# The last pair's pooled mixture loaded in parts, one of them straight from SBUF, with the value steps queued behind the first output products

## The chip, the cores and the metric

One NeuronCore of a Trainium2 chip runs the whole layer. The metric is device microseconds of one execution. The engines keep their own names here: PE (TensorE matmul) with its weight loads (PEld), DVE (VectorE), ACT (ScalarE), POOL (GpSimd) and SP (SyncE, which here only issues DMAs). Each engine has one placed order of instructions; that order is what the change moves.

## The reference, cut to what matters

One decoder layer over 1024 tokens of width 1024, all in float32:

```python
h = x @ w_in                           # columns: pool | q | k | v | forget gate
pool_out = pool_mixer(u, pool_w, pool_scale)      # 4 channel groups, trailing means over 2, 4, 8, 16 tokens
attn_out = forgetting_attention(q, k, v, f_logit) # 8 heads of 64, causal, decay bias
x = layer_norm(alpha * x + concat(pool_out, attn_out) @ w_out)
x = layer_norm(alpha * x + square(relu(x @ w_mlp1)) @ w_mlp2)
```

`concat(pool_out, attn_out)` is called the mixture here. It has 8 channel groups of 128: groups 0 to 3 are the pooled ones, groups 4 to 7 are the four pairs of heads.

## The kernel before, in words

A float32 product is made of three fast ones: every operand is split into a high part (an ACT copy that rounds) and a low part (a DVE subtraction), and `three` issues high x high, high x low, low x high (lines 83 to 85). Products of 512 columns into one PSUM bank are the unit of PE's work.

The mixture goes through a DRAM tensor, `mix_dram`, laid out as four blocks of 256 tokens; each block holds for 128 partitions 8 groups x 256 tokens. Pooled groups 1 to 3 ("early") are written there long before the last pair of heads. Pooled group 0 ("late", window 2) is computed in two halves of 512 tokens (`late_group`), each followed by its small linear map (`late_linear`, line 466: three products, an ACT scaling into the tile `mx`, a store to `mix_dram` at line 471).

Attention runs over pairs of heads, in blocks of 256 queries. A unit of it has two parts: `att_probs` (scores on PE at lines 369, 370 and 372, a running minimum on DVE at line 375, the exponent on ACT at line 377) and `att_values` (transposes at line 397, a high copy on ACT at 398, a low subtraction on DVE at 399, value products at 416, then a store of the result at 423). The units are pipelined by one: values of one unit stand between the probabilities of the next.

Between these steps `fillstep` draws other PE work from a generator, at a rate that spreads the pieces over the last eight units. For the last pair (units with p = 3) the generator is `last_fill` (line 475): the late pooled group in two halves, the loads of the output weights `w_out` (lines 512 and 516), then `mixture(0, 0)` and `mixture(0, 1)` (line 521: a load of four groups of one block, for half 1 also two loads of the softmax row scales from `rin_dram` at line 529 and a DVE multiplication at line 530, then a split), then the output products of the first two token tiles (`out_proj`, line 535): for each tile eight `three`s that need half 0 of the mixture (k = 0 to 3, for both halves of the columns) and eight that need half 1 (k = 4 to 7). `normed` (line 552) adds the residual and normalises; its square root needs another ACT table than the exponent.

A scheduler places all instructions, engine by engine, from its own idea of their durations, so the order on an engine isn't that of the source text. SBUF slots come from small rings by tag (S 3, U 2, B 14, Q 10, A 9): a tile that reuses a slot waits for the last reader of the tile before.

Of the kernel before, what the change touches and what calls it, by code (L numbers as in the profile page):

```python
# [1 line left out]

# [34 lines left out]
def trunk(ctx, tc, xT, xn, wuqk, wvf, bf, poolw, pscale, wout, g1, b1, w1, w2, g2, b2, out):  # L37
# [43 lines left out]
    def three(dst, a, b, first, last):  # L81

        nc.tensor.matmul(dst, a[0], b[0], start=first, stop=False)
        nc.tensor.matmul(dst, a[0], b[1], start=False, stop=False)
        nc.tensor.matmul(dst, a[1], b[0], start=False, stop=last)


    ident = small([P, P], "ident")
# [291 lines left out]
    def att_values(p, e, m, prob, ahead):  # L380
        h = 2 * p + e
        rows = slice(e * HD, (e + 1) * HD)
        orow = slice((1 - e) * HD, (2 - e) * HD)
        ov = bank("pv")[:, 0:256]

        def turned(jp):
            tp = bank("pt")
            tt = slot("A", [2, CH])
            if jp < m:
                blocks = [(jj * 256 + ii * P, 2 * jp + jj, ii) for jj in range(2) for ii in range(2)]  # L390
                ev = slice(0, CH)
            else:
                blocks = [(P, 2 * jp + 1, 1), (2 * P, 2 * jp, 0), (3 * P, 2 * jp, 1)]
                ev = slice(P, CH)
                nc.gpsimd.memset(tt[:, :, 0:P].bitcast(F32), 0.0)
            for col, j, ii in blocks:
                nc.tensor.transpose(tp[:, col : col + P], prob[ii][:, j * P : (j + 1) * P], ident)  # L397
            nc.scalar.copy(tt[:, 0, ev], tp[:, ev])  # L398
            nc.vector.tensor_tensor(tt[:, 1, ev], tp[:, ev], tt[:, 0, ev].bitcast(F32), ALU.subtract)  # L399
            return tt  # L400

        nxt = turned(0)
        next(ahead, None)
        for jp in range(m + 1):
            tt = nxt
            if jp < m:
                nxt = turned(jp + 1)
            if jp == (m + 1) // 2:
                run(ahead)
            fillstep()  # L410
            mov = ((0, 256), (256, CH)) if jp < m else ((256, CH), (0, 256))
            for s in range(2):
                for jj in range(2):
                    j = 2 * jp + jj
                    a, b = mov[jj]
                    nc.tensor.matmul(  # L416
                        ov, V[j][:, h].rearrange("p s d -> p (s d)"), tt[:, s, a:b],
                        start=(j == 0 and s == 0), stop=(j == 2 * m + 1 and s == 1),
                    )
        mx = slot("U", [256], F32)  # L420
        nc.scalar.copy(mx[rows], ov[orow])
        nc.vector.tensor_tensor(mx[rows], ov[rows], mx[rows], ALU.add)
        nc.sync.dma_start(mix_dram[m, rows, NG + p, :], mx[rows])
        if p == NPAIR - 1:
            row_scales(h, 2 * m, 2)
        elif m == 0:
            row_scales(h, 0, NT)
# [37 lines left out]

    def late_linear(c, pw):
        y, mx = pooled.pop(c)
        dst = bank("mm")
        three(dst, (pw[:, 0], pw[:, 1]), (y[:, 0], y[:, 1]), True, True)
        nc.scalar.activation(mx, dst, AF.Copy, scale=half_scale)  # L470
        nc.sync.dma_start(
            mix_dram[2 * c : 2 * c + 2, :, LATE, :].rearrange("m p t -> p m t"), mx.rearrange("p (m t) -> p m t", m=2)
        )

    def last_fill():
        w = load_w(wuqk[LATE])
        st = slot("S", [P], F32)
        nc.sync.dma_start(st, poolw[:, LATE])
        pw = slot("U", [2, P])
        split(pw[:, 0], pw[:, 1], st)  # L480
        nc.vector.tensor_scalar(half_scale, ps_sb[:, LATE : LATE + 1], 0.5, None, ALU.mult)
        yield from late_group(0, w)
        load_output_weights(0, 4)
        yield from late_group(1, w)
        late_linear(0, pw)
        yield
        load_output_weights(4, KT)
        load_rows()
        mixture(0, 0)
        mixture(0, 1)  # L490
        pair = slot("B", [2, D], F32)
        for t in range(2):
            xt = pair[:, t]
            nc.sync.dma_start(xt, xn[t])
            yp = [bank("mm") for n in range(2)]
            for half in range(2):
                yield from out_proj(t, yp, range(4 * half, 4 * half + 4))
                if t == half == 0:
                    late_linear(1, pw)
                    yield  # L500
            normed(t, xt, yp)

    wo = {}
# [13 lines left out]
                wo[block] = (hi[:, k], lo[:, k])  # L517

    mixes, done = {}, []

    def mixture(m, half):

# [12 lines left out]
    def out_proj(t, yp, ks):  # L535
        ts_ = slice((t % 2) * P, (t % 2 + 1) * P)
        for n, part in enumerate(yp):
            ns = slice(n * CH, (n + 1) * CH)
            for k in ks:
                a, w = mixes[t // 2, k // 4], wo[k]  # L540
                three(part, (a[0][:, k % 4, ts_], a[1][:, k % 4, ts_]), (w[0][:, ns], w[1][:, ns]), k == 0, k == KT - 1)
                yield

    gb = []

# [16 lines left out]
    class Norm:  # L562
# [53 lines left out]
        def by_three(self):  # L616
# [4 lines left out]
            for c, x in zip(self.cols, self.x):  # L621
# [2 lines left out]
                nc.gpsimd.tensor_tensor(y, y, self.gam[:, c], ALU.mult)  # L624
                nc.gpsimd.tensor_tensor(y, y, self.bet[:, c], ALU.add)
                nc.sync.dma_start(self.store[:, c], y)
    fill = {"gen": iter(()), "credit": 0.0, "rate": 0.0}

    def fillstep():
        fill["credit"] += fill["rate"]  # L630
        while fill["credit"] >= 1.0:
            fill["credit"] -= 1.0
            next(fill["gen"], None)

    order = [(p, e, m) for p in range(NPAIR - 1) for e in range(2) for m in (3, 2, 1, 0)]
    order += [(NPAIR - 1, e, m) for m in range(4) for e in range(2)]
# [622 lines left out]
```

## Time and profile before

| what | us |
|---|---|
| median of 3 runs | 1039.18 (1038.84 to 1039.32) |
| the profiled execution, its own time | 1040.64 |
| its span from the first to the last instruction | 1038.9 |
| PE busy | 1018.5 (98%) |
| DVE busy | 756.6 (73%) |
| ACT busy | 513.6 (49%) |
| POOL busy | 155.0 (15%) |

The profiled execution is 1.46 us slower than the median of the runs; its span leaves 1.74 us outside. Times inside the trace count from the span's start. In the rows of a timeline stand: start, duration, engine, line, operation, output and inputs with the buffer numbers left out, the count of merged instructions, and in brackets how long the engine was idle before and what ended that. The rows of a view by stages hold, for each engine, busy time and count of instructions.

### The profile page before, as it was taken

How to read it: one execution, taken by the hardware profiler on the slowest of the kernel's cores; microseconds unless marked ns; L12 is line 12 of the kernel's file. 1: busy time of each engine (PE TensorE's matmuls, PEld its weight loads, DVE VectorE, ACT ScalarE, POOL GpSimd, SP SyncE). 2: the span in 40 equal slices, each digit the busy share in tenths (PEclk: the TensorE clock that was granted, in tenths of full speed). 3: DMA queues.
4: the chain of work that ended last, by engine and by line, in shares of the span. 5: the costliest groups of instructions: out<-in, count | busy, mean ns of one | idle time of the engine just before them, and what ended most of it. 6: DMA issues, size and time to landing. Idle time of an engine off the chain costs nothing.

```text
span 1038.9 us, 14121 instructions
## 1 busy us (share of the span) xinstructions
PE 1018.5 (98%) x4976; PEld 846.5 (81%) x4976; DVE 756.6 (73%) x1300; ACT 513.6 (49%) x823; POOL 155.0 (15%) x267
## 2 busy tenths in 40 slices
PE   9999999999989999999999999999999999999996
PEld 9988887888767888787888888888878888888884
DVE  4777678677767887989888778788885666565547
ACT  4523566666665332676666766768621211122152
POOL 0200112112100031112122122120100000000047
PEclk9999999999999999999999999999999999999998
DMA  9702311111584532139767567565999888878753
GB/s 359 273 28 82 111 65 32 36 47 54 173 281 140 185 122 99 61 125 353 275 229 276 224 253 273 217 265 184 346 316 321 283 258 283 275 222 269 242 186 121
DMA packets 113671, 206.30 MB, mean 199 GB/s; under 512 B 9592, under 2 KB 78008, under 8 KB 113600
## 3 DMA queue, kind: packets, MB, share of 16 engines
q1 hardware_dynamic: 94608, 137.63, 40.5%
q0 software_dynamic: 18560, 67.12, 16.7%
q8 instruction: 39, 0.64, 0.2%
q10 hardware_dynamic: 432, 0.66, 0.2%
q14 instruction: 32, 0.26, 0.1%
HBM read 132.42 MB, written 72.94 MB: 198 GB/s over the span
## 4 chain that ended last, share of the span: by engine, by line
PE 49%; issue 4%; DVE 3%; DMA 2%; POOL 1%; ACT 0%; DVEq 0%; POOLq 0%; SPq 0%
PE s L1060 15%; PE pv L1060 8%; PE s L727 8%; PE mm L727 6%; PE pt L727 6%; PE pv L727 4%; PE pt L1060 2%; PE mm L1060 2%; DMA S<-in_w_dram 2%; DVE B L72 1%; DMA hid_dram<-A 1%; POOL hid_dram L852 0%; POOL A L720 0%; DVE A L850 0%; DVE bns L573 0%
## 5 line engine op out<-in xcount | busy, mean ns | idle before, releaser
L71 ACT CAST B<-S 128x1024 fp32r<-128x1024 f32 (+1 forms) x78 | 67.7, 881 | 169.4 <-DMA S<-in_w_dram 67.5
L727 PE MATMUL s<-B,Q 128*128 128x512 f32 x492 | 116.4, 389 | 0.2 <-ACT B L71 0.2
L727 PEld LDWEIGHTS s<-B,Q 128*128 128x128 f32 x492 | 92.3, 188 | 19.8 <-ACT B L71 0.6
L72 DVE TENSOR_TENSOR B<-S,B 128x1024 fp32r<-128x1024 f32 (+1 forms) x78 | 78.0, 1008 | 34.0 <-ACT B L71 33.9
L1060 PE MATMUL s<-B,Q 128*128 128x512 f32 x402 | 98.2, 390 | 0.0
L1060 PEld LDWEIGHTS s<-B,Q 128*128 128x128 f32 x402 | 75.5, 188 | 16.2
L71 ACT CAST Q<-S 128x1024 fp32r<-128x1024 f32 x53 | 55.7, 1051 | 58.0 <-PE s L727 17.0
L852 POOL DMA_DIRECT2D hid_dram<-A x90 | 48.1, 537 | 221.5 <-ACT A L849 164.6
L1060 PE MATMUL s<-B,A 128*128 128x512 f32 x321 | 79.7, 393 | 0.0
L72 DVE TENSOR_TENSOR Q<-S,Q 128x1024 fp32r<-128x1024 f32 x53 | 65.6, 1238 | 15.3 <-ACT Q L71 14.8
L727 PE MATMUL pt<-B,Q 128*128 128x512 f32 x312 | 74.6, 389 | 0.0
L727 PE MATMUL mm<-B,Q 128*128 128x512 f32 x300 | 71.6, 389 | 0.0
L1060 PEld LDWEIGHTS s<-B,A 128*128 128x128 f32 x321 | 60.3, 188 | 13.5
L727 PEld LDWEIGHTS pt<-B,Q 128*128 128x128 f32 x312 | 58.5, 188 | 12.1
L727 PEld LDWEIGHTS mm<-B,Q 128*128 128x128 f32 x300 | 56.3, 188 | 11.7
L377 ACT ACTIVATE A<-A,nm 128x1024 f32<-128x1024 f32 (+7 forms) x64 | 49.7, 778 | 32.3 <-DVE nm L375 31.1
L416 PE MATMUL pv<-A,B 128*128 128x256 f32 x320 | 62.2, 295 | 2.7 <-DVE A L399 1.3
L416 PEld LDWEIGHTS pv<-A,B 128*128 128x128 f32 x320 | 51.0, 188 | 17.1 <-ACT A L398 6.9
L399 DVE TENSOR_TENSOR A<-pt,A 128x512 fp32r<-128x512 f32 (+1 forms) x80 | 49.6, 634 | 15.2 <-ACT A L398 14.4
L850 DVE TENSOR_TENSOR A<-A,A 128x1024 f32<-128x1024 f32 x45 | 53.6, 1219 | 0.0
L362 POOL TENSOR_TENSOR A<-A,maskb 128x128 f32<-128x128 f32 x48 | 23.5, 492 | 190.8 <-DVE nm L375 131.8
L398 ACT CAST A<-pt 128x512 fp32r<-128x512 f32 (+1 forms) x80 | 41.4, 542 | 19.3 <-PE pt L397 18.4
(427 smaller groups left out, 2341.7 us busy)
## 6 DMA issues: line engine op xcount, KB each, us to landing
hid_dram<-A POOLq DMA_DIRECT2D x105, 512.0 KB, 4.0
S<-in_w_dram SPq DMA_DIRECT2D x62, 512.0 KB
Q<-hid_dram SPq DMA_DIRECT2D x98, 256.0 KB
A<-hid_dram SPq DMA_DIRECT2D x82, 256.0 KB
S<-in_wuqk_dram SPq DMA_DIRECT2D x12, 512.0 KB
wo_dram<-Q POOLq DMA_DIRECT2D x10, 512.0 KB, 3.8
B<-wo_dram SPq DMA_DIRECT2D x10, 512.0 KB
Q<-hid_dram SPq DMA_DIRECT2D x39, 128.0 KB
```

The source lines that it names most:

```text
L71: nc.scalar.copy(hi, src)
L72: nc.vector.tensor_tensor(lo, src, hi.bitcast(F32), ALU.subtract)
L362: nc.gpsimd.tensor_tensor(nb[:, qs], nb[:, qs], maskb, ALU.add)
L377: nc.scalar.activation(pt[:, :nk], pt[:, :nk], AF.Exp, bias=nm, scale=-1.0, accum_out=rsum[h][:, i : i + 1])
L398: nc.scalar.copy(tt[:, 0, ev], tp[:, ev])
L399: nc.vector.tensor_tensor(tt[:, 1, ev], tp[:, ev], tt[:, 0, ev].bitcast(F32), ALU.subtract)
L416: nc.tensor.matmul(ov, V[j][:, h].rearrange("p s d -> p (s d)"), tt[:, s, a:b], start=(j == 0 and s == 0), stop=(j == 2 * m + 1 and s == 1),)
L727: nc.tensor.matmul(dst, b[x][:, k], A[a][y][:, k], start=first and k == 0 and i == 0, stop=k == H - 1 and i == 2, skip_group_check=not first,)
L850: nc.vector.tensor_tensor(x, x, hi.bitcast(F32), ALU.subtract)
L852: nc.gpsimd.dma_start(hid_dram[self.u, :, i, AT[name] : AT[name] + 2 * CH], part.rearrange("p q n t -> p (q n t)"))
L1060: nc.tensor.matmul(dst, h[:, p_], w[q_], start=first and u == self.us[0] and j == 0, stop=u == self.us[-1] and j == 2, skip_group_check=no ...
```

## The change

- `last_fill` now calls `early_mixture` at its start: groups 1 to 3 of half 0 of the first token block are loaded and split at once (768 columns), into tiles made for all four groups.
- `late_linear(0)` is called inside the second half of the late group, after five of its eight pieces, and no longer behind it. It splits the first 256 columns of its result from `mx`, in SBUF, into group 0 of those tiles; the store to `mix_dram` stays, since the second token block still reads it. So `mixture(0, 0)` is gone as a load.
- `late_linear(1)` takes a PSUM bank of the scores (`s`, 3 banks) in place of one of `mm` (2 banks).
- `mixture(0, 1)` is called behind `late_linear(1)`, after the first eight output pieces.
- `three` returns its last instruction, `out_proj` yields it, and `fillstep` keeps the latest of the first eight that it sees. The value products of an attention step are then placed behind that instruction on PE: an order on the same engine, no semaphore.

```diff
@@ three
-        nc.tensor.matmul(dst, a[1], b[0], start=False, stop=last)
+        return nc.tensor.matmul(dst, a[1], b[0], start=False, stop=last).ins
@@ att_values
-            for s in range(2):
-                ...
+            with tc.issue_after(fill["piece"]) if fill["piece"] else nullcontext():
+                for s in range(2):
+                    ...
@@ late_linear
-        dst = bank("mm")
+        dst = bank("s" if c else "mm")
...
+        if c == 0:
+            hi, lo = mixes[0, 0]
+            split(hi[:, LATE], lo[:, LATE], mx[:, 0:256])
@@ last_fill
+        early_mixture()
         yield from late_group(0, w)
         load_output_weights(0, 4)
-        yield from late_group(1, w)
-        late_linear(0, pw)
-        yield
+        for n, _ in enumerate(late_group(1, w)):
+            yield
+            if n == 4:
+                late_linear(0, pw)
+                yield
         load_output_weights(4, KT)
         load_rows()
-        mixture(0, 0)
-        mixture(0, 1)
...
                 if t == half == 0:
                     late_linear(1, pw)
                     yield
+                    mixture(0, 1)
@@ new
+    def early_mixture():
+        mf = slot("S", [4, 256], F32)
+        nc.sync.dma_start(mf[:, 1:4], mix_dram[0, :, 1:4, :])
+        hi, lo = slot("Q", [4, 256]), slot("Q", [4, 256])
+        split(hi[:, 1:4], lo[:, 1:4], mf[:, 1:4])
+        mixes[0, 0] = (hi, lo)
@@ out_proj
-                three(part, ...)
-                yield
+                yield three(part, ...)
@@ fillstep
-            next(fill["gen"], None)
+            piece = next(fill["gen"], None)
+            if piece and fill["pieces"] < 8:
+                fill["piece"], fill["pieces"] = piece, fill["pieces"] + 1
```

Where the placed order differs, place one: PE in the first units of the last pair, a few rows behind the small linear map of the first late half. In a row stand the line, the operation, the output tile, its inputs and the size; `s` are scores, `pt` transposes, `pv` values, `mm` with B and Q inputs are output products (B a weight, Q the mixture). Before:

```order
L397 MATMUL pt_3307<-ident_63,A_3206 128x128
L397 MATMUL pt_3307<-ident_63,A_3180 128x128
L397 MATMUL pt_3307<-ident_63,A_3206 128x128
L369 MATMUL s_3326<-Q_2364,Q_2365 128x512
L416 MATMUL pv_3285<-A_3287,B_389 128x256 x2
L370 MATMUL s_3326<-Q_2364,Q_2366 128x512
L369 MATMUL s_3331<-Q_2364,Q_2365 128x256
L370 MATMUL s_3331<-Q_2364,Q_2366 128x256
L372 LDWEIGHTS identb_68
L372 MATMUL s_3331<-maskb_70,identb_68 128x128
L416 MATMUL pv_3285<-A_3287,B_389 128x256 x2
L416 MATMUL pv_3285<-A_3308,B_402 128x256 x2
```

Now:

```order
L85 MATMUL mm_3272<-B_3115,Q_2989 128x512
L417 MATMUL pv_3277<-A_3279,B_389 128x256 x4
L369 MATMUL s_3318<-Q_2364,Q_2365 128x512
L370 MATMUL s_3318<-Q_2364,Q_2366 128x512
L369 MATMUL s_3323<-Q_2364,Q_2365 128x256
L370 MATMUL s_3323<-Q_2364,Q_2366 128x256
L372 LDWEIGHTS identb_68
L372 MATMUL s_3323<-maskb_70,identb_68 128x128
L83 MATMUL mm_3272<-B_3115,Q_2988 128x512
L84 MATMUL mm_3272<-B_3116,Q_2988 128x512
L85 MATMUL mm_3272<-B_3115,Q_2989 128x512
L83 MATMUL mm_3273<-B_3105,Q_2988 128x512
```

Before, scores, transposes and values follow each other without other work until the first output product, some 70 rows behind the linear map. Now the first 24 output products (eight pieces) are spread between these steps, and the values stand behind them in groups of four.

Place two: SP, the loads of the first token block's mixture and of its row scales (S tiles from `mix_dram` and `rin_dram`), with what stands ahead of them. Before:

```order
L471 DMA mix_dram<-Q_2986 128x2x256
L516 DMA B_3253<-wo_dram 128x1024
L516 DMA B_3254<-wo_dram 128x1024
L549 DMA B_3259<-in_g_dram 128x1024
L549 DMA B_3259<-in_b_dram 128x1024
L524 DMA S_3262<-mix_dram 128x1024
L524 DMA S_3268<-mix_dram 128x1024
L529 DMA S_3270<-rin_dram 64x4x256 x2
L494 DMA B_3278<-in_xn_dram 128x1024
```

Now:

```order
L562 DMA B_3267<-in_g_dram 128x1024
L562 DMA B_3267<-in_b_dram 128x1024
L499 DMA B_3270<-in_xn_dram 128x1024
L424 DMA mix_dram<-U_3340 64x256
L437 DMA rin_dram<-row_3348 2x128
L538 DMA S_3421<-mix_dram 128x1024
L543 DMA S_3423<-rin_dram 64x4x256
L472 DMA mix_dram<-Q_3123 128x2x256
L543 DMA S_3423<-rin_dram 64x4x256
L424 DMA mix_dram<-U_3448 64x256
```

The load for half 0 is gone from here, the load for half 1 stands one store and one 512 KB load (`in_xn_dram`) further back, and the store of the second late half has come between the two loads of row scales.

Place three: ACT, from the exponent table's reload to the exponent that needs it, with the waits of each row in brackets. Before:

```order
L398 CAST A_3603<-pt_3602 128x512 [waits PE_49]
L377 ACT_TABLE_LOAD
L377 ACTIVATE A_3589,rsum_2973<-A_3589,nm_3599 128x896 [waits DVE_49]
L398 CAST A_3621<-pt_3620 128x512 [waits PE_49]
L398 CAST A_3639<-pt_3638 128x384 [waits PE_49]
L71 CAST Q_3980<-S_3978 128x1024 [waits DMAHW5_49,DMAHW1_49]
```

Now:

```order
L398 CAST A_3605<-pt_3604 128x512 [waits PE_49]
L71 CAST Q_3800<-S_3794 128x1024 [waits DMAHW4_49,DVE_49]
L398 CAST A_3623<-pt_3622 128x512 [waits PE_49,Activation_49]
L398 CAST A_3641<-pt_3640 128x384 [waits PE_49]
L71 CAST Q_3982<-S_3980 128x1024 [waits DMAHW7_49]
L377 ACT_TABLE_LOAD [waits DVE_49,Activation_49]
L377 ACTIVATE A_3648,rsum_2973<-A_3648,nm_3658 128x1024 [waits Pool_49]
L422 COPY U_3681<-pv_3582 64x256 [waits DMAHW6_49,PE_49]
```

Before, the reload has no wait of its own and the exponent of 896 columns follows it. Now the exponent of 1024 columns follows it, and its waits (for the minimum on DVE among others) stand on the reload.

More of the change, by code (lines that the diff above doesn't have):

```diff
@@ L1 @@
-from contextlib import ExitStack
+from contextlib import ExitStack, nullcontext
 import concourse.bass as bass
@@ L411, in att_values @@
             mov = ((0, 256), (256, CH)) if jp < m else ((256, CH), (0, 256))
-            for s in range(2):
[L413 to L419, printed above, removed]
+            with tc.issue_after(fill["piece"]) if fill["piece"] else nullcontext():
+                for s in range(2):
+                    for jj in range(2):
+                        j = 2 * jp + jj
+                        a, b = mov[jj]
+                        nc.tensor.matmul(
+                            ov, V[j][:, h].rearrange("p s d -> p (s d)"), tt[:, s, a:b],
+                            start=(j == 0 and s == 0), stop=(j == 2 * m + 1 and s == 1),
+                        )
         mx = slot("U", [256], F32)
@@ L540, in out_proj @@
                 a, w = mixes[t // 2, k // 4], wo[k]
-                three(part, (a[0][:, k % 4, ts_], a[1][:, k % 4, ts_]), (w[0][:, ns], w[1][:, ns]), k == 0, k == KT - 1)
-                yield
+                yield three(part, (a[0][:, k % 4, ts_], a[1][:, k % 4, ts_]), (w[0][:, ns], w[1][:, ns]), k == 0, k == KT - 1)
     gb = []
@@ L626, in by_three @@
                 nc.sync.dma_start(self.store[:, c], y)
-    fill = {"gen": iter(()), "credit": 0.0, "rate": 0.0}
+    fill = {"gen": iter(()), "credit": 0.0, "rate": 0.0, "piece": None, "pieces": 0}
     def fillstep():
```

## The prediction

> **What bounds the kernel now.** First the view by stages. Columns: stage, its length, then busy us and (instructions) of PE, PEld, DVE, ACT, POOL, the granted clock, the DMA share, GB/s.
>
> ```profile
> 271.40:289.10 17.70, 17.43 (x98) 13.47 (x96) 12.81 (x36) 12.10 (x33) 1.94 (x5) 1.00 0.75 255
> 289.10:303.50 14.40, 12.07 (x77) 9.20 (x75) 10.20 (x30) 9.58 (x20) 1.66 (x4) 1.00 0.91 295
> 303.50:315.10 11.60, 11.11 (x49) 8.33 (x48) 6.94 (x14) 5.69 (x9) 0.00 (x0) 1.00 0.69 194
> 315.10:344.10 29.00, 28.14 (x162) 23.50 (x162) 24.95 (x46) 16.29 (x28) 1.76 (x4) 1.00 0.48 150
> ...
> 344.10:400.00 55.90, 55.90 (x270) 46.80 (x269) 42.83 (x76) 14.10 (x26) 12.32 (x14) 1.00 0.38 134
> ...
> 400.00:450.00 50.00, 49.66 (x228) 40.57 (x227) 45.00 (x76) 25.17 (x44) 9.17 (x8) 1.00 0.25 85
> 450.00:500.00 50.00, 48.82 (x216) 40.08 (x215) 44.88 (x57) 38.78 (x48) 11.69 (x21) 1.00 0.76 284
> ...
> 600.00:1000.00 400.00, 399.55 (x1751) 328.23 (x1750) 275.60 (x375) 162.13 (x212) 31.99 (x51) 1.00 0.79 265
> ```
>
> PE is the bound nearly everywhere: from 600 to 1000 us it idles 0.45 us. The last pair is an exception. From 289.1 to 303.5 it idles 2.33 us, in the two stages behind it 0.49 and 0.86. That, 3.7 us, is all that an order of the same instructions can win here, plus what each wait costs beyond its idle time. PE's rows of the first gap show what it waits for:
>
> ```profile
> 288.28 0.48 PE L83 MATMUL mm<-Q,U 128*128 128x512 f32 x1
> ...
> 290.52 0.48 PE L369 MATMUL s<-Q,Q 128*128 128x512 f32 x1
> 291.65 0.50 PE L416 MATMUL pv<-A,B 128*128 128x256 f32 x2 [0.66 <-ACT A L398]
> ...
> 295.60 0.87 PE L397 MATMUL pt<-ident,A 128*128 128x128 f32 x6 [0.36 <-ACT A L377]
> 296.82 0.50 PE L416 MATMUL pv<-A,B 128*128 128x256 f32 x2 [0.35 <-ACT A L398]
> ...
> 301.27 0.55 PE L397 MATMUL pt<-ident,A 128*128 128x128 f32 x3 [0.32 <-ACT A L377]
> 302.07 0.50 PE L369 MATMUL s<-Q,Q 128*128 128x512 f32 x1 [0.25 <-DVE nm L375]
> ...
> 303.28 0.33 PE L397 MATMUL pt<-ident,A 128*128 128x128 f32 x1 [0.41 <-DVE A L399]
> 303.50 0.50 PE L83 MATMUL mm<-B,Q 128*128 128x512 f32 x1
> ...
> 304.07 0.39 PE L83 MATMUL mm<-B,Q 128*128 128x512 f32 x1
> 304.30 0.39 PE L84 MATMUL mm<-B,Q 128*128 128x512 f32 x1
> ...
> 310.47 0.50 PE L83 MATMUL mm<-B,Q 128*128 128x512 f32 x1 [0.42 <-ACT Q L71]
> ...
> 325.39 0.66 PE L397 MATMUL pt<-ident,A 128*128 128x128 f32 x4 [0.80 <-ACT row L435]
> ```
>
> Between the late half's linear map (288.28) and the first output product (303.50) PE has attention alone, and each step of it (scores, minimum, exponent, transposes, split, values) waits for the last. A wait costs more than its idle time: after a product of 512 columns the next starts 0.23 us later (304.07 to 304.30), but 290.52 to 291.65 is 1.13, a loss of 0.90 for 0.66 idle, a factor of 1.4.
>
> The output products come so late because of loads. These are SP's issues and the first users on ACT and DVE:
>
> ```profile
> 293.74 1.02 SPq L524 DMA_DIRECT2D S<-mix_dram  x2
> 294.82 1.68 SPq L529 DMA_DIRECT2D S<-rin_dram  x2
> ...
> 302.39 1.05 ACT L71 CAST Q<-S 128x1024 fp32r<-128x1024 f32 x1
> ...
> 303.67 1.22 DVE L72 TENSOR_TENSOR Q<-S,Q 128x1024 fp32r<-128x1024 f32 x1
> ...
> 308.12 1.23 DVE L530 TENSOR_TENSOR S<-S,S 128x1024 f32<-128x1024 f32 x1 [1.08 <-issue]
> 309.38 1.05 ACT L71 CAST Q<-S 128x1024 fp32r<-128x1024 f32 x1 [0.98 <-DVE S L530]
> ```
>
> Half 0 is issued at 293.74 and split at 302.39; the row scales of half 1 are issued from 294.82 and used at 308.12, with DVE idle ahead of it. The DMA share is 0.91 in that stage: these loads stand in a full queue.
>
> **The change, part by part.** *The early part and the direct part of half 0.* The single split of 1024 columns becomes 768 plus 256: by the rows above (1.05 on ACT, 1.22 on DVE, at 1024) some 0.2 us more on each in all. Of it, 768 columns come in front of a DVE queue that idles:
>
> ```profile
> 266.82 0.29 DVE L375 CUSTOM_DVE_ANT_0 A<-s,A 128x128 f32<-128x128 f32 x1 [0.48 <-PE s L370]
> ...
> 267.75 0.20 DVE L431 RECIPROCAL ri<-rsum 128x8 f32<-128x8 f32 x1 [0.62 <-ACT A L377]
> 268.23 0.68 DVE L336 SCALAR_TENSOR_TENSOR Q<-mm,Q 64x512 fp32r<-64x512 f32 x1 [0.28 <-ACT Q L335]
> ```
>
> Three quarters of 1.22 is 0.92 us, against 1.38 idle: nothing, or 0.5 at most if the exponent next to it takes the delay on. The load is 384 KB in place of 512 and leaves the full queue; the store stays.
>
> *The first eight pieces.* The 24 output products (24 x 0.23 = 5.5 us) now stand between the steps of the gap, and the linear map no longer waits for the end of the late group. No wait of the gap is longer than 0.66, and a piece is 0.69, so they cover it: minus 2.35 x 1.4 = 3.3 us. The order of values behind pieces is on PE itself and sets no wait. The wait of 0.42 at 310.47 is for the load of half 1, that of 0.80 at 325.39 for a copy on ACT queued behind a split that waited for row scales; in the new order the transposes there stand behind a copy that ACT reaches well earlier. Both are written off, 1.22 x 1.4 = 1.7. Removed in all: 5.0.
>
> *What is left without cover.* From the second linear map to the first product of half 1 the new order has attention alone again: 20 values (0.12 each), 10 scores of 512 columns (0.23), 4 of 384, 16 transposes (0.11) and the changes between them, about 8 us against some 11 us of work in the old gap. At the old rate (3.3 over 11) the loss is 2.4; but scores here run two units ahead of their values, so that a value's inputs are mostly done. I walked the three queues through it with the durations above. What remains is one place: DVE takes the multiplication by row scales (1.23) and only then the low split of the last transposes (0.5), which PE needs 0.9 us earlier. With its factor 1.3, and 0.2 for a value behind the POOL subtraction that now holds ACT early in the gap: 1.5, between 0.6 and 2.4.
>
> *The row scales.* Half 1's loads are now ready to issue at about 298, and the second load of row scales, behind the store of the late half, at about 304 (the linear map ends near 302, the ACT scaling takes 0.69). DVE arrives near 309. From issue to use such a pair takes:
>
> ```profile
> 313.19 1.28 SPq L529 DMA_DIRECT2D S<-rin_dram  x2
> ...
> 316.08 0.69 ACT L470 ACTIVATE Q<-mm,hsc 128x512 f32<-128x512 f32 x1 [3.25 <-PE mm L85]
> ...
> 320.71 1.23 DVE L530 TENSOR_TENSOR S<-S,S 128x1024 f32<-128x1024 f32 x1 [0.74 <-DMA S<-rin_dram]
> ...
> x_dram<-A POOLq DMA_DIRECT2D x12, 256.0 KB, 2.5
> ```
>
> The last of the pair, issued at 313.83, is used at 320.71, so 6.9 us with the mixture's 512 KB just ahead; 256 KB of another kind land in 2.5. The load in question is 256 KB with its companions long gone, so I take the lower part, 4 us: landing at 308, no wait. By the upper end DVE waits 2 us, and PE with it. Between 0 and 2; I take 0.
>
> *The exponent behind the table.* In the old order the table goes back to the exponent's before its input is ready, as the first two rows show:
>
> ```profile
> 323.08 1.28 ACT L580 ACT_TABLE_LOAD   x1
> 324.38 0.29 ACT L580 ACTIVATE rt<-mv,eps 128x1 f32<-128x1 f32 x1
> ...
> 326.69 1.28 ACT L377 ACT_TABLE_LOAD   x1
> 329.06 1.05 ACT L377 ACTIVATE A<-A,nm 128x896 f32<-128x896 f32 x1 [1.08 <-DVE nm L375]
> ...
> 334.32 1.15 ACT L377 ACTIVATE A<-A,nm 128x1024 f32<-128x1024 f32 x1
> ```
>
> In the new one the reload itself waits for the minimum on DVE, so 1.28 + 1.15 follow it in a row, and the copy that frees a transpose bank stands behind. DVE reaches this minimum after the second multiplication by row scales, the normalisation of tile 0 and three splits, some 9 us after tile 0's statistics. By my walk the exponent ends 0.6 us after PE wants it, and the copy adds 0.3: 0.9, between 0 and 2.5. The page "ScalarE: Activation LUTs" of the Trainium skill ("What ACT_TABLE_LOAD costs") gives about 2.66 us for a switch, 1.28 of load and 1.38 of drain; here the square root starts 0.02 us after the load's end (323.08 + 1.28, 324.38), so no run here shows the drain. By the page the exponent would be 1.4 later and the gain 1.4 us.
>
> *The bank.* Scores have two banks for the time that ACT takes to read the late half, 0.69 us; the next score in that bank stands two scores later. Nothing, or 0.3.
>
> *The sum.* Minus 5.0, plus 1.5, plus 0, plus 0.9, plus some 0.2 for the splits: minus 2.4 by idle times. Starts of PE's rows one by one, against the dense rows, give a little more loss in the old order (many waits below 0.1 us aren't marked as idle), so I take minus 2.8. From 344.1 on PE is full, and what follows is started by its products, so the shift should reach the end. The profiled execution, 1040.64 (span 1038.9, 1.74 around it), would take 1037.8; it is 1.46 above the median of the runs, so against 1039.18 I predict 1036.4.
>
> **The rivals.** *The stall only moves.* The uncovered stretch loses at the old rate (2.4), the late exponent costs 1.7 (halfway from its 0.9 to the upper end), or DVE, which is busy for 90 of the 100 us from 400 to 500, doesn't follow PE's earlier start. For it: each wait of the gap is for ACT or DVE, and they get no less work. Against: 8.5 us of idle DVE between 375 and 400 (the row of that stage below). Sum: minus 5.0 plus 2.4 plus 1.7 plus 0.2, minus 0.7: 1038.5.
>
> ```profile
> 375.00:400.00 25.00, 25.00 (x126) 21.03 (x125) 16.48 (x33) 5.11 (x11) 3.25 (x6) 1.00 0.17 64
> ```
>
> *DVE is held by the row scales (slower).* The multiplication stands in DVE's queue ahead of all minima and low splits of the next units. In the old order its second load took from 295.6 to 308.1, 12.5 us. Were it so again, it would land at 316.6 in place of 308: DVE, there at 309, 7.6 us late, PE as much, and minus 2.8 becomes plus 4.8: 1044.0. The gain is gone from 7.6 us between issue and landing on (the slack up to it, 4.8, plus 2.8). For it: the second load waits for a store that waits for PE. Against: in the new order the loads of w_out, g and b stand six and more issues ahead of it on SP, and its own issue waits until 304. The page "TensorE: Matmul & The Clock Gate" ("What's actually happening") adds that an idle window of about 3.4 us halves PE's clock; the granted clock is 1.00 in all stages above, whose longest wait is 0.80, so no run here shows it.
>
> *More is won.* Uncovered stretch 0.6, exponent 0, and the small waits below 0.1 go as well: minus 5.0 plus 0.6 plus 0.2, minus 1: 1034.0.
>
> That the change doesn't do what it says is excluded: the placed order shows the products where they should be.
>
> **How the numbers follow.** The forecast has 0.58, with its own range from 1035.2 to 1037.8 (the bounds of the stretch and the exponent); the stall that moves 0.26, the held DVE 0.08, the larger gain 0.08. Leaving out the upper half of the held DVE and the end of the larger gain, the range is 1034.3 to 1039.8. 0.2% is 2.1 us, about what a measurement of this kernel can tell from no change. Below 1037.1 lie the larger gain and five sixths of the forecast, 0.56; above 1041.3 the held DVE, 0.08, and 0.01 of unnamed mishaps; the rest is 0.35.
>
> **What would show it.** Right: from 289 to 301 PE idles under 0.5 us with output products between the attention steps; 1 to 1.5 us of idle time around 302 to 312, the largest before a value product that waits for DVE line 399; a wait of transposes for the exponent near 330; PE full again some 3 us before 344. Wrong: a multiplication by row scales that waits more than 2 us for its DMA; idle PE between 400 and 500 grown by over 1 us; an idle sum in the last pair above 2.5 us.

## The result and the profile after

The changed kernel takes 1041.51 us, the median of nine runs (1040.25 to 1042.98), and the kernel before 1039.01 in runs of the same job (1038.01 to 1040.04). The ratio is 1.0024 (1.0016 to 1.0033): 2.5 us slower, where 2.8 us of gain were forecast. The profiled execution took 1042.98, with a span of 1041.2.

The same stages as in the prediction, for the kernel after (columns as there; the granted clock is the third number from the end):

```profile
271.40:289.10 17.70, 17.60 (x102) 14.23 (x101) 12.96 (x33) 12.93 (x32) 1.81 (x5) 1.00 0.81 262
289.10:303.50 14.40, 14.33 (x88) 12.19 (x88) 8.42 (x25) 8.53 (x18) 1.75 (x4) 1.00 0.86 298
303.50:315.10 11.60, 8.88 (x48) 7.30 (x47) 8.45 (x19) 6.75 (x14) 0.31 (x1) 0.87 0.65 179
315.10:344.10 29.00, 26.51 (x134) 21.97 (x134) 23.59 (x40) 14.32 (x21) 1.45 (x3) 0.94 0.45 130
```

The old gap is filled: PE's idle time between 289.1 and 303.5 fell from 2.33 us to 0.07. In its place the two stages behind it idle 2.72 and 2.49 us, where they idled 0.49 and 0.86, and the granted clock is below 1.00, as in no stage of the kernel before ahead of its last. PE's rows at both places, and one row far behind them:

```profile
308.27 0.40 PE L370 MATMUL s<-Q,Q 128*128 128x512 f32 x1
311.32 0.51 PE L417 MATMUL pv<-A,B 128*128 128x256 f32 x2 [2.65 <-DVE A L399]
...
312.48 0.63 PE L84 MATMUL mm<-B,Q 128*128 128x512 f32 x1
312.91 0.63 PE L83 MATMUL mm<-B,Q 128*128 128x512 f32 x1
...
336.01 0.39 PE L84 MATMUL mm<-B,Q 128*128 128x512 f32 x1
338.71 0.51 PE L417 MATMUL pv<-A,B 128*128 128x256 f32 x2 [2.31 <-DVE A L399]
...
351.64 0.39 PE L84 MATMUL mm<-B,Q 128*128 128x512 f32 x1
```

Two value products wait 2.65 and 2.31 us for a low split on DVE (line 399). Behind the first wait, products of 512 columns start 0.43 us apart (312.48 to 312.91) in place of 0.23: that is the half clock. The product at 351.64 is the one that started at 349.75 in the kernel before, so 1.9 us of delay are there already. That row of the kernel before:

```profile
349.75 0.39 PE L84 MATMUL mm<-B,Q 128*128 128x512 f32 x1
```

What DVE and SP did, for the first wait and then for the second:

```profile
307.80 0.08 DVE L375 DVE_READ_ACCUMULATOR2_ANT nm<- 128x1 f32 x1
309.57 1.23 DVE L544 TENSOR_TENSOR S<-S,S 128x1024 f32<-128x1024 f32 x1 [1.69 <-DMA S<-rin_dram]
310.72 0.55 DVE L399 TENSOR_TENSOR A<-pt,A 128x384 fp32r<-128x384 f32 x1
...
327.94 1.22 DVE L72 TENSOR_TENSOR Q<-S,Q 128x1024 fp32r<-128x1024 f32 x1
...
336.83 1.23 DVE L544 TENSOR_TENSOR S<-S,S 128x1024 f32<-128x1024 f32 x1 [3.06 <-DMA S<-rin_dram]
```

```profile
302.13 0.37 SPq L472 DMA_DIRECT2D mix_dram<-Q  x1
302.54 0.60 SPq L543 DMA_DIRECT2D S<-rin_dram  x1
...
329.24 1.25 SPq L543 DMA_DIRECT2D S<-rin_dram  x2
```

DVE is done with its work at 307.9 and stands for 1.69 us before the multiplication by row scales (line 544), because the load issued at 302.5, behind the store of the late half (line 472), has not landed. The low split that PE wants stands behind that multiplication. The second time the loads are issued at 329.24, when the split that began at 327.94 has freed a staging buffer (1.22 us later), and DVE stands for 3.06 us.

The clock, in short windows around both waits:

```profile
308.00:310.00 2.00, 0.67 (x4) 0.23 (x2) 0.43 (x1) 1.24 (x2) 0.25 (x1) 1.00 1.00 364
310.00:312.00 2.00, 0.68 (x6) 0.67 (x6) 1.43 (x4) 1.14 (x2) 0.00 (x0) 1.00 0.47 178
312.00:314.00 2.00, 2.00 (x8) 1.51 (x7) 1.94 (x3) 0.53 (x2) 0.00 (x0) 0.50 0.69 242
314.00:316.00 2.00, 2.00 (x8) 1.71 (x7) 1.44 (x4) 1.53 (x2) 0.00 (x0) 0.64 0.21 56
...
340.00:342.00 2.00, 2.00 (x10) 1.91 (x9) 1.68 (x3) 1.87 (x3) 0.00 (x0) 0.50 0.00 0
```

After each wait PE runs at half the clock. The trace's clock records give the stretches: 3.41 us from 312.01, 3.41 us from 339.32. Starts of PE's rows, taken one by one against the mean of the same pairs of rows where PE is full, give an estimate of the bill between 271 and 350 us: the kernel before lost some 7.8 us there, the kernel after 9.8. Of the 9.8, 2.8 and 2.5 are the two waits and 1.8 and 1.7 the slow rows behind them, 8.8 together; all the rest is 1.0. So the old places gave some 6.8 us, more than the 5.0 that the prediction took off, and 8.8 us were lost at two new places. The level depends on the price taken for a full pair (with the median in place of the mean both sums are some 3 us higher); the difference of 2.0 and the four terms hardly do.

### The profile page after: what moved, and what is told of

It reads as the page before. It is cut to its first block, busy times and chain, and to the rows that moved or that the text cites. A ratio compares the mean times of both kernels' runs of the same rounds, so it can differ in the third digit from the quotient of the medians.

```text
span 1041.2 us, 14129 instructions
## 1 busy us (share of the span) xinstructions
PE 1019.1 (98%) x4976; PEld 848.4 (81%) x4976; DVE 757.0 (73%) x1301; ACT 514.6 (49%) x824; POOL 155.4 (15%) x267
## 4 chain that ended last, share of the span: by engine, by line
PE 49%; issue 4%; DVE 3%; DMA 2%; POOL 1%; SPq 0%; ACT 0%; DVEq 0%; POOLq 0%
PE s L1075 15%; PE pv L1075 8%; PE s L742 8%; PE mm L742 6%; PE pt L742 6%; PE pv L742 4%; PE pt L1075 2%; PE mm L1075 2%; DMA S<-in_w_dram 1%; DMA hid_dram<-A 1%; DVE B L72 1%; POOL hid_dram L867 0%; POOL A L735 0%; DVE A L865 0%; SPq L1054 0%
## 5 line engine op out<-in xcount | busy, mean ns | idle before, releaser
L71 ACT CAST Q<-S 128x1024 fp32r<-128x1024 f32 (+1 forms) x53 | 55.5, 1047 | 57.0 <-PE s L742 17.0
L72 DVE TENSOR_TENSOR Q<-S,Q 128x1024 fp32r<-128x1024 f32 (+1 forms) x53 | 65.3, 1233 | 13.9 <-ACT Q L71 13.6
```

The costliest lines, as they stand in the source:

```text
L71: nc.scalar.copy(hi, src)
L72: nc.vector.tensor_tensor(lo, src, hi.bitcast(F32), ALU.subtract)
```

## Experiments

My theory after the result: a load of row scales takes 5 to 7 us wherever it stands, the change puts PE's work earlier against it, and the multiplication that waits for it holds the low splits behind it on DVE; the half clock adds to each long wait. Rivals: DVE has no time to spare and the wait would only move; the half clock alone is the loss; the gain was never there. Each median stands beside that of the kernel before from the same job.

| run | edit | us | before | ratio |
|---|---|---|---|---|
| e1 | the changed kernel again | 1044.17 | 1039.23 | 1.0042 (1.0030 to 1.0054) |
| e2 | half 1 called early | 1036.90 | 1039.23 | 0.9982 (0.9971 to 0.9992) |
| e3 | multiplication on POOL | 1046.94 | 1039.23 | 1.0070 (1.0057 to 1.0083) |
| e4 | e2 and e3 | 1041.88 | 1039.23 | 1.0028 (1.0009 to 1.0048) |
| e5 | 4 KB packets | 1035.98 | 1039.50 | 0.9969 (0.9956 to 0.9981) |
| e6 | e2 and e5 | 1036.07 | 1039.50 | 0.9972 (0.9960 to 0.9983) |
| e7 | kernel before, 4 KB packets | 1038.40 | 1039.50 | 0.9996 (0.9985 to 1.0007) |
| e8 | e2, half 0 through DRAM | 1041.23 | 1039.50 | 1.0017 (1.0008 to 1.0026) |
| e9 | half 1 just ahead of the second map | 1036.97 | 1038.74 | 0.9985 (0.9976 to 0.9993) |
| e10 | e9 and e5 | 1034.56 | 1038.74 | 0.9960 (0.9947 to 0.9972) |
| e11 | e5, first map late | 1036.30 | 1038.74 | 0.9970 (0.9959 to 0.9981) |
| e12 | e5, half 0 through DRAM | 1039.98 | 1038.74 | 1.0014 (1.0005 to 1.0023) |
| e13 | 1 KB packets of own addresses | 1036.11 | 1039.26 | 0.9971 (0.9961 to 0.9981) |
| e14 | 4 KB packets of own addresses | 1036.27 | 1039.26 | 0.9972 (0.9960 to 0.9983) |

### e1: the changed kernel again

> The changed kernel itself, timed more often, since some of its executions show two stretches of 3.4 us at a granted clock of 0.5 and some show none (mean clocks of its runs so far from 0.993 to 0.997). My theory: the loss is two PE waits of 2.65 and 2.31 us behind the multiplication by row scales, plus the half clock that follows some of them; the time should be 1.002 to 1.003 of the kernel before, and runs of mean clock 0.993 or 0.994 slower than runs of 0.997 by 1.0 to 3.0 us. Rival 1, the half clock alone is the loss: runs at 0.997 equal to the kernel before within 0.5 us. Rival 2, the half clock costs nothing, as DVE is the bound behind the wait anyway: runs at 0.993 and 0.997 equal within 0.5 us.

1.0042 of the kernel before, more than in the result. In three executions the mean clock is 0.994: 1044.17, 1044.40 and 1045.52; the first of them is the profiled one, and its trace has the two stretches of half clock. In two it is 0.997, as in the kernel before: 1042.35 and 1042.41. The difference of the means is 2.3 us; in the nine runs of the result it is 1.3 (1042.64 for the three at 0.993 and 0.994, 1041.38 for the four at 0.997). Without the half clock the kernel is still 2.4 to 3.2 us slower than the one before, so the first rival falls and the waits are the larger part. That the half clock costs something is clear in e1; in the nine runs the two groups overlap, and the two runs at 0.995 (1041.04 and 1040.78) are among the fastest. The load of the first place took 7.5 us in e1's trace and PE's wait was 3.23, which may be part of why e1 is slower than the result.

### e2: half 1 called ahead of the first output products

```diff
         load_rows()
+        mixture(0, 1)
         pair = slot("B", [2, D], F32)
...
                     late_linear(1, pw)
                     yield
-                    mixture(0, 1)
```

> Only mixture(0, 1) is called where it was before the change, ahead of the first output products, so that its loads are issued ahead of the store of the late half. My theory: the first wait (2.65 us before a value product) goes, the second (2.31) stays; 2.8 us and the half clock behind it are won, so about 1038.0 (1037 to 1039). Rival, DVE has no time to spare here and the wait only moves: 1041 to 1042.

1036.90, 7 us below e1 in the same job, a little below what I expected, and the kernel is faster than the one before. The first wait shrank to 0.87 us and, unlike what I expected, the second to 0.91:

```profile
307.02 0.66 PE L397 MATMUL pt<-ident,A 128*128 128x128 f32 x4 [0.87 <-DVE A L399]
335.39 0.50 PE L417 MATMUL pv<-A,B 128*128 128x256 f32 x2 [0.91 <-DVE A L399]
```

The wait did not move elsewhere: DVE has the time. The loads of the second place, the row scales for token tiles 4 and 5, are issued at 327.07 here, 2.2 us earlier than in the changed kernel, since the split that frees their buffer comes earlier.

### e3 and e4: the multiplication on POOL

```diff
-            nc.vector.tensor_tensor(mf, mf, rb, ALU.mult)
+            nc.gpsimd.tensor_tensor(mf, mf, rb, ALU.mult)
```

> Only the engine of the multiplication by row scales changes, from DVE to POOL (2.4 us for 128x1024 by POOL's rows of that shape, against 1.23). My theory: low splits no longer queue behind it, so the second wait goes (minus 2.5 us and its half clock); at the first place half 1 itself becomes late by 1.2 us, and an output product waits some 3 us in place of the value product: about 1038.0 (1036.5 to 1039.5). Rival, the load is what PE waits for wherever the multiplication stands: both waits stay and grow by 1.2 us each, 1043 to 1045.

> Both edits. My theory: both waits go, and with them the half clock: 1041.5 minus 2.8 minus 2.5 minus 1 to 3 for the clock, about 1034.5 (1033 to 1036.5), below the kernel before. Rival, the waits only move: 1039 to 1042.

My theory failed on e3: 1046.94, above even the rival's 1043 to 1045. Rows of POOL and ACT around its second long wait, and PE's rows behind both:

```profile
339.91 2.36 POOL L544 TENSOR_TENSOR S<-S,S 128x1024 f32<-128x1024 f32 x1 [9.34 <-DMA S<-rin_dram]
```

```profile
342.30 1.04 ACT L71 CAST Q<-S 128x1024 fp32r<-128x1024 f32 x1 [4.89 <-POOL S L544]
```

```profile
313.77 0.80 PE L83 MATMUL mm<-B,Q 128*128 128x512 f32 x1 [3.45 <-ACT Q L71]
...
343.88 0.50 PE L417 MATMUL pv<-A,B 128*128 128x256 f32 x2 [2.88 <-ACT A L398]
```

With DVE free, the next instruction that needs half 1 holds its own queue: the high split on ACT stands 4.89 us, and the high copy of the transposes (line 398), for which PE waits, stands behind it. The block goes with the late load from engine to engine; it is the load that has to be earlier. It failed on e4 too: 1041.88, where 1034.5 was expected. With the loads early, the longest wait of its profiled execution (1038.39) is 1.58 us, again for the split of half 1 on ACT, and the multiplication's extra 1.2 us stay:

```profile
308.73 0.50 PE L83 MATMUL mm<-B,Q 128*128 128x512 f32 x1 [1.58 <-ACT Q L71]
```

Its runs spread from 1038.25 to 1051.15. The three slowest (1044.77, 1046.40, 1051.15) have the lowest mean clocks, 0.991 to 0.994 against 0.995 to 0.997 in the others, so stretches of half clock come with them; what makes their waits longer, no trace shows.

### e5 and e6: the row scales in runs of 4 KB

```diff
-    rin_dram = dr.tile([NH, S], F32, name="rin_dram")
+    rin_dram = dr.tile([2, NT // 2, NPAIR, 256], F32, name="rin_dram")
...
-        nc.sync.dma_start(rin_dram[h, i * P : (i + n) * P].rearrange("(i q) -> i q", q=P), row[0:n])
+        dst = rin_dram[h % 2, i // 2 : (i + n) // 2, h // 2, :].rearrange("m (u q) -> m u q", q=P)
+        nc.sync.dma_start(dst, row[0:n])
...
-                rows = rin_dram[e::2, m * 256 : (m + 1) * 256].rearrange("(o p) t -> o p t", o=1)
+                rows = rin_dram[e, m : m + 1]
```

> The changed kernel with one thing else: the row scales lie in DRAM so that a load reads one run of 4 KB for each partition (64 packets) in place of four of 1 KB (256 packets). The order of all engines is the same as without it. My theory: the row-scale loads are slow by themselves, whatever the queue holds (5 to 7 us from issue to landing in every place of the traces, the last 1 KB packets taking 0.1 to 0.27 us each); with 4 KB packets the load issued at 302.4 lands near 306 and that at 329.7 near 333, both waits of DVE go: 1038 (1036 to 1039.5), granted clock 1.00 in the last pair. Rival, what is late is the place in the queue behind the late half's store and the mixture: landing still after 308, 1041.5 to 1044.

> Half 1 called early as in the run before (1036.9) and the 4 KB packets. My theory: its two waits that are left (0.87 and 0.91 us, behind the multiplication by row scales) go in part, one of them was a wait of DVE for the load (1.45): 1035.8 (1034.5 to 1036.9). Rival: with half 1 early no load is late any more, same as 1036.9 within 0.7.

e5 is the cleanest of the runs: every engine has the same instructions in the same order as the changed kernel, only the addresses in DRAM differ. It takes 1035.98, 0.9969 of the kernel before, just below the expected range. The second load is issued at 303.44 and lands at 307.36: 3.9 us, where it took 6.9. The stages and the waits of e5:

```profile
303.50:315.10 11.60, 10.66 (x62) 8.64 (x61) 9.91 (x23) 8.62 (x17) 0.31 (x1) 1.00 0.65 207
315.10:344.10 29.00, 29.00 (x156) 24.26 (x155) 26.06 (x47) 15.28 (x24) 2.52 (x5) 1.00 0.48 146
```

```profile
310.43 0.51 PE L417 MATMUL pv<-A,B 128*128 128x256 f32 x2 [0.87 <-DVE A L399]
```

```profile
331.25 1.23 DVE L545 TENSOR_TENSOR S<-S,S 128x1024 f32<-128x1024 f32 x1 [0.37 <-DMA S<-rin_dram]
```

One wait above 0.25 us is left on PE in these stages, 0.87 us, and the clock is 1.00. The second wait is gone though its loads are still issued only when the buffer is free: the later of the two takes 4.2 us, DVE stands 0.37 us, and PE has other work meanwhile.

e6 is no better than e2 or e5 alone (1036.07). The time is as expected, but the waits that were to go didn't all go: in its profiled execution, the slowest of its runs (1037.82), the loads, issued at 292.9 and 293.4 into a full queue, take 12.6 and 13.1 us, and PE waits again behind the multiplication:

```profile
308.50 1.12 PE L397 MATMUL pt<-ident,A 128*128 128x128 f32 x4 [2.52 <-DVE A L399]
```

### e7: the kernel before with 4 KB packets

> The kernel before with the 4 KB packets alone. My theory: there the output products wait for the mixture of half 0, which stands ahead of the row scales in the queue, and DVE waits for row scales by only 1.08 and 0.74 us: 1038.7 (1037.7 to 1039.3). Rival, row scales bound the gap of the kernel before as well: 1036 to 1037.5.

The edit is that of e5, on the kernel before: 0.9996 (0.9985 to 1.0007), no difference. With the new layout on both sides the change wins 2.4 us (1035.98 against 1038.40, same job). But the layout hardly makes the loads quicker here, so e7 doesn't test a quick load without the change. The later load of the first pair takes 12.0 us from issue to landing (12.5 in the kernel before), that of the next pair 6.4 (6.7). Both pairs are issued just behind the mixture's 512 KB.

### e8, e11 and e12: parts of the change undone

In e8 (on e2) and e12 (on e5) half 0 goes wholly through DRAM again: early_mixture and the split out of SBUF go, and mixture(0, 0) is called behind load_rows. In e11 (on e5) the first linear map stands behind the whole second late group.

```diff
-        early_mixture()
...
-        if c == 0:
-            hi, lo = mixes[0, 0]
-            split(hi[:, LATE], lo[:, LATE], mx[:, 0:256])
...
         load_rows()
+        mixture(0, 0)
```

```diff
-        for n, _ in enumerate(late_group(1, w)):
-            yield
-            if n == 4:
-                late_linear(0, pw)
-                yield
+        yield from late_group(1, w)
+        late_linear(0, pw)
+        yield
```

> Half 1 called early, the late half's first linear map early as in the change, but half 0 of the first mixture wholly through DRAM again (one load of 512 KB behind the store, one split of 1024 columns). My theory: the direct part is what lets the products start at 290; without it they start some 8 us later and the idle time of 2.33 us of the kernel before comes back: 1038.5 (1037.7 to 1040). Rival, the early linear map alone does it, or what counts is only where half 1 stands: 1036.9 within 0.7.

> 4 KB packets, and the other part undone: half 0 wholly through DRAM, half 1 where the change puts it. My theory: the direct part is the change's gain; without it the attention steps of the gap wait again: 1039.5 (1038 to 1041.5). Rival, with fast loads the way through DRAM is early enough: 1036 to 1037.5.

> 4 KB packets, and one part of the change undone: the first linear map of the late half stands behind the whole second late group again (half 0 still partly straight from SBUF). My theory: the products start some 3 us later, and one or two attention steps lose their cover: 1037 (1036 to 1038.5). Rival, six products of the late group more or less ahead of the map make no difference: 1036.0 within 0.7.

Without the early and the direct part e8 takes 1041.23 (e2: 1036.90; by the ratios 1.0017 against 0.9982) and e12 1039.98 (e5: 1035.98; 1.0014 against 0.9969), each pair from two jobs. e8 is slower than expected (1038.5, up to 1040), slower even than the kernel before; why, stays open. The gap is back in e12, with the product that ends it waiting for the split of a half 0 that came through DRAM:

```profile
289.10:303.50 14.40, 10.79 (x55) 6.62 (x54) 9.10 (x25) 8.73 (x18) 1.75 (x4) 1.00 0.95 330
```

```profile
292.10 0.51 PE L369 MATMUL s<-Q,Q 128*128 128x512 f32 x1 [0.99 <-DVE nm L375]
...
302.11 0.50 PE L83 MATMUL mm<-B,Q 128*128 128x512 f32 x1 [1.04 <-ACT Q L71]
```

e11 takes 1036.30, a ratio of 0.9970 against the 0.9969 of e5, as its rival had it: where the first map stands makes no difference that these runs show, once its result goes straight from SBUF. The early load and the direct split together are the gain, some 4 us; they were not undone one by one.

The ordering of value steps behind pieces has no run of its own: without that line the instructions of all five engines are placed in the same order, in the changed kernel and in e2, so this part of the change does nothing here. The change of the second map's bank was not tried alone.

### e9 and e10: half 1 ahead of the second linear map

```diff
                 if t == half == 0:
+                    mixture(0, 1)
                     late_linear(1, pw)
                     yield
-                    mixture(0, 1)
```

> The changed kernel with 1 KB packets as it was; mixture(0, 1) is called just ahead of the second linear map of the late half in place of just behind it, so that its second row-scale load stands on SP ahead of the store of the late half and not behind it. My theory: the first late load is late for two reasons, issue behind the store (302.4 where 298 was possible) and 6.9 us of its own; taking the first away lands it near 304.5, the first wait shrinks from 2.65 to 0.9 or less and the second (2.31) stays: 1041 (1039.5 to 1042.5). Rival, the packets alone decide and the place on SP doesn't matter: 1042.5 to 1044.5 (the changed kernel took 1041.5 and 1044.2 on two chips).

> The same order with 4 KB packets. My theory: both causes of the late load gone; of the 0.87 us left before a value product nothing was a wait for the load, so little is won: 1035.8 (1034.8 to 1036.6). Rival, the earlier place of the multiplication on DVE takes the 0.87 away: 1034 to 1035.

e9, with 1 KB packets, takes 1036.97, 0.9985 of the kernel before; I had expected 1041. Its rows:

```profile
298.14 1.31 SPq L543 DMA_DIRECT2D S<-rin_dram  x2
```

```profile
309.09 0.51 PE L417 MATMUL pv<-A,B 128*128 128x256 f32 x2 [0.54 <-DVE A L399]
322.18 0.51 PE L417 MATMUL pv<-A,B 128*128 128x256 f32 x2 [0.90 <-DVE A L399]
336.64 0.50 PE L417 MATMUL pv<-A,B 128*128 128x256 f32 x2 [0.76 <-DVE A L399]
```

Both loads go out together at 298 and land at 304.3 and 305.6, still 6 to 7 us each, and DVE doesn't wait for them at 307. As in e2 the later waits shrink with the first, to 0.90 and 0.76: too short for the half clock. e10, with both cures, takes 1034.56, 0.9960 (0.9947 to 0.9972), the lowest of all, 4.2 us below the kernel before in the same job, 2.4 below e9. One wait is left:

```profile
309.14 0.51 PE L417 MATMUL pv<-A,B 128*128 128x256 f32 x2 [0.54 <-DVE A L399]
```

That is below what I expected and fits the rival, that the earlier place on DVE takes from the last wait (0.87 in e5). Against e5 (0.9969, 0.9956 to 0.9981) the intervals overlap, so the two aren't told apart.

### e13 and e14: what makes the load slow

```diff
-                rows = rin_dram[e::2, m * 256 : (m + 1) * 256].rearrange("(o p) t -> o p t", o=1)
-                nc.sync.dma_start(rb[e * HD : (e + 1) * HD], rows.to_broadcast([HD, NPAIR, 256]))
+                rows = xn[0:NPAIR, 0:HD, 0:256].rearrange("j p t -> p j t")
+                nc.sync.dma_start(rb[e * HD : (e + 1) * HD], rows)
```

(e14: `rows = xn[e, 0:HD, :].rearrange("p (j t) -> p j t", t=256)`.)

> The changed kernel with the row-scale loads reading an input of the same size in place of the row scales, for timing alone: 256 packets of 1 KB for each load, but each from its own address, where the real load reads the same 4 KB for all 64 partitions. The order is as in the changed kernel. If the 256 packets are the price: landing 6 to 7 us after issue again, and 1041 to 1044. If all partitions reading one place is the price: landing in 3.5 to 4.5 us, and 1035.5 to 1037.

> The same with 64 packets of 4 KB, each from its own address; the values are again not the row scales. With 4 KB packets of one address the load took 3.7 to 4.2 us. If the address matters at all: 2.5 to 3.2 us; if not: 3.7 to 4.2 as well. Time 1035.5 to 1037 either way.

Both kernels leave out the row scales, which the results lack; they serve for the time alone. The load that first came late, in four kernels whose engines have the same order, by the trace's records of issue and landing, and the later one of the pair that came late the second time:

| packets | address | kernel | issue, landing | takes | second place takes |
|---|---|---|---|---|---|
| 256 of 1 KB | the same four runs of 1 KB for all 64 partitions | after | 302.54, 309.45 | 6.9 | 6.8 |
| 64 of 4 KB | the same run of 4 KB for all 64 partitions | e5 | 303.44, 307.36 | 3.9 | 4.2 |
| 256 of 1 KB | its own for each | e13 | 302.58, 306.08 | 3.5 | 4.1 |
| 64 of 4 KB | its own for each | e14 | 303.03, 306.54 | 3.5 | 4.2 |

It is neither the number of packets nor the shared address alone, but small packets that all read one place. (e13 and e14 read another tensor as well; 1 KB packets of one address from there were not run.) The 3.5 us of e14 lie between its two expectations (2.5 to 3.2, and 3.7 to 4.2). In the changed kernel the median 1 KB packet took 0.05 us when the load began and 0.27 at 306.5; in e13 the medians stay at 0.05.

The form decides only away from the mixture's load. The first row-scale load of the same pair is issued 0.4 us behind the mixture's 512 KB, and there all four forms take long: 5.6 us in the changed kernel, 7.0 in e5, 6.0 in e13, 6.5 in e14. In the same way the two loads that e10 issues together take 7.6 and 8.0 us with 4 KB packets, against 6.2 and 6.7 in e9 with 1 KB.

The times follow the load that first came late: 1036.11 and 1036.27, like e5. DVE in e13 finds its load landed, and PE's one wait is the one of e5:

```profile
307.84 1.22 DVE L544 TENSOR_TENSOR S<-S,S 128x1024 f32<-128x1024 f32 x1
```

```profile
309.58 0.51 PE L417 MATMUL pv<-A,B 128*128 128x256 f32 x2 [0.88 <-DVE A L399]
```

The Trainium skill, "DMA: Bandwidth & Descriptors" ("Specifications"), has transfers run at line rate from 512 bytes on. For packets with addresses of their own the runs agree (3.5 us for 1 KB and for 4 KB); for packets of one address they don't (6.9 against 3.9).

## Why the prediction was wrong

**The first eight pieces: right.** They were to cover the waits of the gap, 2.35 us idle and 3.3 with the changes around them; the stage's idle time fell from 2.33 us to 0.07. That the shift reaches the end held too, with the other sign: 1.9 us at 351.64, 1.8 at 960.

**What is left without cover: right in place and size, once the load is quick.** The one place named, the multiplication by row scales ahead of the low split that PE needs 0.9 us earlier, is the 0.87 us of e5. The exponent behind the table was priced too high: by its starts PE lost 0.2 us there, where 0.9 was taken:

```profile
330.40 1.28 ACT L377 ACT_TABLE_LOAD   x1 [1.90 <-DVE nm L375]
331.69 1.16 ACT L377 ACTIVATE A<-A,nm 128x1024 f32<-128x1024 f32 x1
```

```profile
332.54 0.40 PE L85 MATMUL mm<-B,Q 128*128 128x512 f32 x1
332.99 1.33 PE L397 MATMUL pt<-ident,A 128*128 128x128 f32 x7
```

The exponent starts 0.01 us after the load's end, so the drain that the Trainium skill's page on "ScalarE: Activation LUTs" adds ("What ACT_TABLE_LOAD costs") is not seen at this place either.

**The row scales: the step that failed.** "I take the lower part, 4 us: landing at 308, no wait." The load took 6.9 and landed at 309.45, the multiplication waited 1.69, and with the 0.9 in front of the low split PE stood 2.65. The row for 6.9 stood in the prediction; I put its length down to the mixture just ahead of it in the queue and went down towards a store of the same size (2.5). For that row the mixture was reason enough: with 4 KB packets the same load of the kernel before still takes 6.4 (e7). But it doesn't follow that the load is quick without the mixture ahead. In the changed kernel it took as long when issued alone, and there the form of its reads set the price: 3.9 in e5, 3.5 in e13. The bound was there ("by the upper end DVE waits 2 us, and PE with it"), and the value was chosen from the row that was least like it. The issue (302.54 for some 304) and DVE's arrival (307.9 for 309) both came earlier than walked; with 4 us there would have been no wait. With quick loads (e5, 3.9) the kernel takes 0.9969 of the one before, 1035.8 against its 1039.01; the forecast was 1036.4. That this is so close is partly luck: the traces of e5 and of the kernel before differ by 4.7 us in place of 2.8, and the profiled execution of the kernel before, from which the terms were read, was 1.46 above its median.

**The same load a second time: not in the prediction.** I followed the multiplication through the first tile pair alone. Every later pair has one. The loads of the third pair wait for a buffer that a split on DVE frees, and PE, now earlier, met them too: 2.31 us. Two signs of being wrong that the prediction named came with it, a multiplication that waits over 2 us for its load (3.06) and an idle sum above 2.5 us (5.2 in the two stages).

**The clock: dismissed on the old rows.** The page "TensorE: Matmul & The Clock Gate" of the Trainium skill was cited for an idle window of 3.4 us and set aside because no wait of the kernel before was above 0.80. The upper end of my own load price gave a wait of 2.9 us (2 of DVE, 0.9 behind it), which no row of the kernel before could judge, and the clock got no term for it. The two stretches cost 1.8 and 1.7 us in the profiled execution, and 1.3 to 2.3 us together between executions with and without them.

**The rivals.** That DVE is held by the row scales was the right mechanism, with a chance of 0.08. Its price was worked out for a landing 12.5 us after issue, and its threshold (gain gone from 7.6 us) left out the second place and the clock; 6.9 us were enough. "The stall only moves" didn't come true: in e5 it doesn't, and DVE keeps up.

## What to carry to other kernels

When work on the bound engine moves earlier, price every load that now stands closer to its use, at each repetition of the loop, with the nearest row of the same kind of load; a row of another kind (here a store) is no price. A load that is read by all partitions from one place should be laid out so that each partition reads one long run: here a change of layout alone turned a change that loses 2.5 us into one that wins 3. It helps where the load doesn't stand right behind another large one; there the layout made loads hardly quicker (6.4 for 6.7 us in e7) or not at all. And an instruction that waits for a late load holds whatever stands behind it on its engine; moving it to another engine moves the block, and issuing the load ahead of a store that waits removes it.

## What the runs showed of the hardware

- Small packets that read one place are slow: 6.9 us for 256 packets of 1 KB from the same four runs of 1 KB, 3.9 for 64 of 4 KB from one run, 3.5 for either size from own addresses (of another tensor). Why, no run shows. Right behind a load of 512 KB the four forms take 5.6, 7.0, 6.0 and 6.5 us.
- In these traces the half clock goes by PE's idle time in one step of a fixed raster, not by the length of a wait. In every trace the half clock begins and ends a whole number of steps of 3.413 us behind the first clock record (in the kernel after, 90 steps to 312.01 and 98 to 339.32), but for the end of the execution; a stretch lasts one step or two (6.83 us in e3). I count PE's idle time by these steps. Those with 1.86 us or more were followed by the half clock: 2.65 and 2.31 here, 3.01 and 2.12 in e1, 1.87, 1.86 and 2.13 in e3, 2.37 in e6. None of the others was, in any of the sixteen traces, and they go up to 1.62 (e3) and 1.58 (e4). So the wait of 2.88 us in e3 wasn't enough by itself: it lies across the end of a step, 1.62 and 1.26, and the half clock came when the wait of 0.87 behind it made 2.13 of the second part. The raster fits the free-running window of 3413 ns in "TensorE: Matmul & The Clock Gate" ("What's actually happening") of the Trainium skill. Its rule of no idle gap above some 3.4 us ("HAM oscillation — how this bites in real kernels") is too mild here. That the same kernel shows the stretches in some executions and not in others would follow from where the steps fall against its waits; the changed kernel's executions without them have no trace.
- A load issued earlier into a full queue hardly lands earlier: issued at 293.44 (e2) the second row-scale load landed at 304.96, issued at 298.84 (e9) at 305.55.
